# fp16 granule pipeline carried from the feed-forward part back to the mLSTM input block

## The chip, the cores and the metric

The kernel runs on one core of one Trainium2 chip. The metric is the device time of one execution in microseconds (us); lower is better. Times of the kernel before: 1895.95, 1896.54 and 1900.0 us, median 1896.54 us. The engines are named as in the profile: PE is TensorE (PEld its weight loads), DVE is VectorE, ACT is ScalarE, POOL is GpSimd, SP is SyncE, from whose queue most weights are fetched.

## The reference

One inference step of one decoder layer for 288 tokens (256 of a prompt, 8 samples of 4), in fp32. The mixer projects the normed input with one wide matrix `w_in` into three parallel branches (RG-LRU, gated linear attention, mLSTM) and into three merge gates, and adds the branches' outputs behind their gates. A squared-ReLU MLP follows.

```python
xn = rmsnorm(x, P['g_norm1']) * (1.0 + sc1) + sh1
proj = xn @ P['w_in']     # 2048 x 12312: lru_x, g_q, g_k, g_v, g_lr, g_gate, m_x, m_o, m_if, mg
y_lru, y_gla, y_ml = ...  # the three recurrences
gate = jax.nn.sigmoid(mg).reshape(B, T, 3, 2048)
merged = gate[:, :, 0] * (y_lru @ P['w_br_lru']) + gate[:, :, 1] * (y_gla @ P['w_br_gla']) \
       + gate[:, :, 2] * (y_ml @ P['w_br_ml'])
x = x + gt1 * (merged @ P['w_out'])
xn = rmsnorm(x, P['g_norm2']) * (1.0 + sc2) + sh2
x = x + gt2 * (jnp.square(jax.nn.relu(xn @ P['w_ff1'])) @ P['w_ff2'])
y = rmsnorm(x, g_final)
```

The shifts, scales and gates `sh1 ... gt2` are products of 9 conditioning rows with `w_ada` (2048 x 12288). The recurrences' new states are outputs too.

## The kernel before

**Layout.** Features lie on the 128 partitions, the 288 tokens along the free dimension. A weight matrix is read in granules: one fetch of 512 KB, a tile of 128 x 1,024, which holds eight 128x128 weight tiles. Every weight and every activation is split into a high and a low part, and each product takes three matmuls (high-high, high-low, low-high), so a granule is 24 matmuls of 128x288.

**Two ways to split.** Up to `wout` the function `stream` (L152 to L192) does it in fp32r: ACT copies the raw granule to `hi` (L160), DVE subtracts it to give `lo` (L162), PE multiplies at L169. It holds three raw, three high and three low tiles. The feed-forward part uses fp16 parts instead, which need a common power-of-two scale for each block of four granules. The class `Block` (L226 to L264) has the steps: `scan` squares a raw granule on ACT and adds it up (L236); `total` sums over the partitions with a ones product on PE into a PSUM bank of its own (L240); `scale` turns the sum into a power of two and its inverse with four small DVE operations (`power_of_two`, L195 to L202) and one that multiplies in the activations' factor (L245); `convert` makes the high part on ACT (L249) or on DVE (L251) and the low part on DVE (L252); `multiply` is L263. The factor is taken out again when the block's PSUM bank is evicted. The feed-forward loop scans ten granules ahead and converts three ahead; fetched granules lie in eleven places.

**Order.** The engines' instructions are put in order when the program is built, by priorities; `in_order` ties a granule step's instructions to the order in which they are written, `issue_after` ties one to another, and SP's queue follows the program. Work beside the streams (the recurrences as Python generators) advances by one piece after each granule (`run`, L272 to L283), and `finish` forces what is left of a piece of work.

**Stages**, with the start in the profiled execution: norm and the LRU, query, key and value blocks (0), the GLA output gate (218), merge 0 (272: four times a gate block and an output block, with LRU and then GLA beside it), the mLSTM input block (485), merge 1 (541, with mLSTM beside), the mLSTM output block (750), merge 2 (806), `wout` (982), feed-forward part (1088). Merge 1 and 2 multiply the gate by the branch's product and add (L1329, L1330); `wout` is evicted by `resid` (L1764 to L1769). At the start of the feed-forward part `second_norm` (L1815 to L1826) makes the 16 tiles of the normed input one by one; each serves the first block as soon as it is there.

**Conditional weights.** The products with `w_ada` are laid between the granules by a schedule written as a string (`every`). One half of each of the shift, scale and gate of the second norm is split into fp16 parts by `cond_parts` (L403 to L450; L411 and L417 on ACT, L419 on DVE, products at L433); the rest are fp32 products (L372).

Of the kernel before, what the change touches and what calls it, by code (L numbers as in the profile page):

```python
# [50 lines left out]
B_LRU, B_Q, B_GATE, B_MX, B_MO, B_MG = 0, 2, 6, 8, 10, 12  # L51
# [3 lines left out]
def trunk(ctx, tc, io):  # L55
# [22 lines left out]
    def slot(i, dt=F32):  # L78
        return big.tile([P, 8, N], dt, tag=f"s{i}", name=nm(f"s{i}"))
# [31 lines left out]
    junk = con[:, 0:512].bitcast(BF16)  # L111
# [40 lines left out]
    def stream(w, blk, act, kt, evac, g0=0, width=512, ahead=True, k0=0, kg=2, behind=None, banks=None):  # L152
# [3 lines left out]
        for g in range(k0 // kg, kt // kg):  # L156
# [28 lines left out]
            for m in range(nm_t):  # L185
# [3 lines left out]
                if g == kt // kg - 1:  # L189
                    with tc.high_priority():  # L190
                        evac(m, pss[m][:, :N])
            yield  # L192


    def power_of_two(p, n, of):  # L195

        q, t, u = (of[:, i:i + 1] for i in (4, 5, 6))
        V.tensor_reduce(out=q, in_=p[:, 0:n], axis=AX.X, op=ALU.add)
        V.tensor_scalar(q.bitcast(I32), q.bitcast(I32), 0x7F000000, 1, ALU.bitwise_and, ALU.logical_shift_right)
        V.tensor_scalar(u.bitcast(I32), q.bitcast(I32), -1, 204 << 23, ALU.mult, ALU.add)  # L200
        V.tensor_scalar(t.bitcast(I32), q.bitcast(I32), 50 << 23, None, ALU.add)
        return t, u  # L202

# [15 lines left out]
    taken = {"n": 0}  # L219

    def bank():

        taken["n"] += 1
        return longp() if taken["n"] % 5 == 0 else pm.tile([P, 512], F32, tag="mm", name=nm("mm"))

    class Block:  # L226

        def __init__(self, w, blk, g0, width, act, back, evac, by_act):
            self.w, self.blk, self.g0, self.act, self.back, self.evac, self.by_act = w, blk, g0, act, back, evac, by_act
            self.nm_t, self.kg = width // P, 1024 // width  # L230
            self.of, self.ps = None, None

        def scan(self, g, raw):
            if g == 0:
                self.of = sc([P, 8], "sums", 4)
            pace["hi"] = S.activation(junk, raw, AF.Square, accum_out=self.of[:, g:g + 1])  # L236

        def total(self):
            self.p = misc()
            T.matmul(self.p[:, 0:4], words(ones, 1, BF16), words(self.of[:, 0:4], 1, BF16), start=True, stop=True)  # L240

        def scale(self):
            t, self.u = power_of_two(self.p, 4, self.of)
            self.c = self.of[:, 7:8]
            V.tensor_tensor(out=self.c, in0=t, in1=self.back(), op=ALU.mult)  # L245

        def convert(self, g, raw, hi, lo):
            if g in self.by_act:
                pace["hi"] = S.activation(hi, raw, AF.Copy, scale=self.u)  # L249
# [3 lines left out]

        def multiply(self, g, hi, lo, ms, kks):
            if self.ps is None:
                self.ps = [bank() for _ in range(self.nm_t)]
# [1875 lines left out]
```

## Time and profile before

| | |
|---|---|
| median of the three runs | 1896.54 us |
| the profiled execution's own time | 1895.68 us |
| its span, first to last instruction | 1893.9 us |
| busy share of the span: PE, DVE, ACT, POOL | 98%, 67%, 59%, 12% |
| granted PE clock, mean | 0.995 |
| moved by DMA | 422.90 MB, 223 GB/s |

Busy time of PE is a union of overlapping instructions: matmuls are pipelined, so the length of one (286 to 301 ns in the groups) is not the time that it adds. The time between two starts is that, and the chain of waits shows it as a length and a count. "L169" is line 169 of the kernel. A row of a window has its start and end, its length, then each engine's busy time and its number of instructions, the granted clock, the DMA engines' busy share and GB/s. A row of waits has who waited for whom, the total, the number and the longest.

### The profile page before, as it was taken

The numbers are of one execution on the slowest core, as the hardware profiler recorded it, in microseconds if no ns is written. First come the engines' busy times: TensorE is split into PE (matmuls) and PEld (weight loads), VectorE is DVE, ScalarE is ACT, GpSimd is POOL, SyncE is SP. The second block draws the span as 40 slices with busy tenths as digits, with TensorE's granted clock in tenths as the row PEclk, the third lists the DMA queues.
The fourth block names the chain that finished last, engine by engine and source line by source line (L and its number), as shares of the span: only waits on it lengthen the run. The fifth ranks groups of instructions, "written<-read, shape, count | busy, mean of one in ns | idle before, by whom it ended". The sixth has DMA issues, their size and how long they took to land.

```text
span 1893.9 us, 38893 instructions
## 1 busy us (share of the span) xinstructions
PE 1847.8 (98%) x15874; PEld 1621.6 (86%) x15874; DVE 1268.2 (67%) x2239; ACT 1117.3 (59%) x1861; POOL 219.9 (12%) x302
## 2 busy tenths in 40 slices
PE   8999999999999999999999979999999999999997
PEld 7998889999999999999999947777777777777775
DVE  4767846645684557776558678776868676767676
ACT  5333374545454444566448568877777766666673
POOL 0001200000123010011101520000000000000091
PEclk9999999999999999999999999999999999999999
DMA  9998666547844358856787656565556555556541
GB/s 384 398 372 301 242 236 240 201 145 260 276 159 168 134 172 296 302 204 223 296 341 298 246 210 222 172 222 185 189 188 203 176 181 168 188 169 188 168 155 51
DMA packets 113442, 422.90 MB, mean 223 GB/s; under 512 B 11808, under 2 KB 12096, under 8 KB 110064
## 3 DMA queue, kind: packets, MB, share of 16 engines
q1 hardware_dynamic: 97040, 361.04, 54.9%
q0 software_dynamic: 11472, 42.79, 6.4%
q10 hardware_dynamic: 4752, 16.60, 2.2%
q8 instruction: 124, 2.03, 0.4%
q14 instruction: 54, 0.44, 0.1%
HBM read 403.56 MB, written 16.81 MB: 222 GB/s over the span
## 4 chain that ended last, share of the span: by engine, by line
PE 80%; DVE 9%; ACT 6%; issue 3%; DMA 1%; POOL 0%; SPq 0%; DVEq 0%; ACTq 0%; POOLq 0%
PE mm L169 39%; PE mm L263 24%; PE pi L263 6%; PE pa L372 3%; DVE pair L252 2%; ACT pair L249 2%; PE px L169 2%; DVE lo L162 1%; ACT con L236 1%; DMA raw<-win 1%; ACT hi L160 1%; PE pa L433 1%; DVE pair L251 0%; DVE s L800 0%; PE px L1649 0%
## 5 line engine op out<-in xcount | busy, mean ns | idle before, releaser
L263 PEld LDWEIGHTS <-pair 128*128 128x128 f16 x6144 | 596.6, 98 | 176.8 <-issue 11.9
L160 ACT ACTIVATE hi<-raw 128x1024 fp32r<-128x1024 f32 x272 | 286.9, 1057 | 407.4 <-PE mm L169 250.4
L162 DVE TENSOR_TENSOR lo<-raw,hi 128x1024 fp32r<-128x1024 f32 x272 | 334.9, 1233 | 248.0 <-ACT hi L160 227.9
L169 PE MATMUL mm<-xh,hi 128*128 128x288 f32 x1440 | 429.4, 301 | 4.0 <-ACT xh L718 1.7
L169 PE MATMUL mm<-xl,hi 128*128 128x288 f32 x1440 | 423.5, 297 | 0.0
L169 PE MATMUL mm<-xh,lo 128*128 128x288 f32 x1440 | 411.9, 296 | 2.0 <-DVE lo L162 1.9
L263 PE MATMUL mm<-x,pair 128*128 128x288 f16 x2448 | 316.1, 287 | 10.1 <-ACT x L1824 6.3
L263 PE MATMUL mm<-hx,pair 128*128 128x288 f16 x2472 | 321.8, 286 | 2.7 <-ACT s L1873 1.4
L169 PEld LDWEIGHTS mm<-xh,hi 128*128 128x128 f32 x1440 | 270.4, 188 | 15.8 <-issue 8.1
L169 PEld LDWEIGHTS mm<-xl,hi 128*128 128x128 f32 x1440 | 270.8, 188 | 1.4
L169 PEld LDWEIGHTS mm<-xh,lo 128*128 128x128 f32 x1440 | 266.0, 188 | 4.9 <-DVE lo L162 2.9
L169 PE MATMUL mm<-s,hi 128*128 128x288 f32 x1280 | 252.8, 297 | 1.1 <-DVE s L1769 0.7
L169 PEld LDWEIGHTS mm<-s,hi 128*128 128x128 f32 x1280 | 201.8, 188 | 5.1 <-issue 2.9
L169 PE MATMUL mm<-s,lo 128*128 128x288 f32 x640 | 179.2, 296 | 1.6 <-DVE lo L162 1.0
L252 DVE SCALAR_TENSOR_TENSOR pair<-xl,sums,pair 128x1024 f16<-128x1024 f32 x92 | 117.8, 1284 | 62.9 <-ACT pair L249 61.6
L252 DVE SCALAR_TENSOR_TENSOR pair<-s,sums,pair 128x1024 f16<-128x1024 f32 x92 | 118.1, 1284 | 52.7 <-ACT pair L249 51.4
L252 DVE SCALAR_TENSOR_TENSOR pair<-raw,sums,pair 128x1024 f16<-128x1024 f32 x72 | 93.2, 1295 | 41.6 <-ACT pair L249 40.6
L169 PEld LDWEIGHTS mm<-s,lo 128*128 128x128 f32 x640 | 116.9, 188 | 2.3 <-DVE lo L162 2.1
L1861 POOL TENSOR_SCALAR s<-s,mod 128x256 f32<-128x256 f32 x16 | 21.5, 1347 | 675.7 <-DVE s L1877 675.7
L236 ACT ACTIVATE con<-s 128x1024 bf16<-128x1024 f32 x92 | 96.3, 1046 | 1.3 <-DMA s<-wf 0.3
L236 ACT ACTIVATE con<-xl 128x1024 bf16<-128x1024 f32 x92 | 96.2, 1046 | 0.9
L263 PE MATMUL pi<-hx,pair 128*128 128x288 f16 x600 | 89.8, 286 | 3.1 <-DVE rs_t L1767 1.8
(526 smaller groups left out, 2275.7 us busy)
## 6 DMA issues: line engine op xcount, KB each, us to landing
raw<-win SPq DMA_DIRECT2D x192, 512.0 KB, 4.4
s<-wf SPq DMA_DIRECT2D x92, 512.0 KB, 3.9
xl<-wf SPq DMA_DIRECT2D x92, 512.0 KB, 4.1
raw<-wf SPq DMA_DIRECT2D x72, 512.0 KB, 3.9
s<-wq SPq DMA_DIRECT2D x20, 1024.0 KB, 8.7
raw<-wout SPq DMA_DIRECT2D x32, 512.0 KB, 5.9
s<-wada SPq DMA_DIRECT2D x13, 1024.0 KB, 7.3
ag<-wada POOLq DMA_DIRECT2D x12, 1024.0 KB, 7.8
```

The source lines that it names most:

```text
L160: pace["hi"] = S.activation(hi, raw, AF.Copy)
L162: pace["lo"] = V.tensor_tensor(out=lo, in0=raw, in1=hi.bitcast(F32), op=ALU.subtract)
L169: pace["last"] = T.matmul(ps, w[:, kk, ms], x, start=k == k0 and i == 0, stop=k == kt - 1 and i == 2)
L236: pace["hi"] = S.activation(junk, raw, AF.Square, accum_out=self.of[:, g:g + 1])
L249: pace["hi"] = S.activation(hi, raw, AF.Copy, scale=self.u)
L252: pace["lo"] = V.scalar_tensor_tensor(lo, raw, self.u, hi, ALU.mult, ALU.subtract)
L263: pace["last"] = T.matmul(self.ps[m][:, :N], a[:, kk, m * P:(m + 1) * P], x, start=k == 0 and i == 0, stop=k == 4 * self.kg - 1 and i == 2)
L372: pace["prod"] = T.matmul(ps[32 * j:32 * j + 32, h * w // 4:(h + 1) * w // 4], stat(k), v[:, j], start=k == 0 and h == 0, stop=k == kt - 1 ...
L433: pace["prod"] = T.matmul(ps[32 * j:32 * j + 32, a:a + 256], c, v[:, j], start=q == i == n == 0, stop=q == KT // each - 1 and n == 1, skip ...
L1861: G.tensor_scalar(a[:, 0:NP], a[:, 0:NP], mod[:, GT2, k, 0:1], None, ALU.mult)
```

## The change

The pipeline of `Block` now starts 40 blocks earlier. One list holds all blocks from the mLSTM input on: 4 of the mLSTM input, then merge 1 (two gate blocks of 256 columns and one output block of 512, four times), 4 of the mLSTM output gate, merge 2 like merge 1, 8 of `wout`, and the feed-forward blocks. `feed` runs through it: in each granule step it converts up to seven granules ahead and scans up to twelve (fourteen in the feed-forward part).

- The normed input `xn` is converted from its fp32r parts to fp16 parts in four groups (`halves16`: POOL adds the parts to one tile, ACT and DVE split it again), beside the first output blocks of merge 0. The buffers of the fp32r parts are cut up so that each can be given on.
- Merge 0 first does all four gate blocks, then all four output blocks. During these sixteen granules, still in fp32r, `ramp` fetches, scans and converts the first granules of the pipeline.
- The branch results and the merged sum are measured and split into fp16 parts (`measured`, `measured_sum`, `merged`) instead of fp32r parts.
- `total` writes into columns 288 and up of the first bank of the block that is being multiplied, between the products of its first and second output tile; in the feed-forward part it keeps a bank of its own.
- The first two feed-forward blocks are multiplied side by side, tile by tile (`by_k`).
- `cond_parts` is gone: all conditional weights are fp32 products. The GLA and the LRU recurrence are one generator, LRU no longer forced after the first gate block.

The core of the diff, shortened:

```diff
-    def stream(w, blk, act, kt, evac, ..., banks=None):
+    def stream(w, blk, act, kt, evac, ..., banks=None, then=None):
...
+            if then:
+                then(g, pss)
             yield
...
         def total(self):
-            self.p = misc()
-            T.matmul(self.p[:, 0:4], words(ones, 1, BF16), words(self.of[:, 0:4], 1, BF16), start=True, stop=True)
+            p = None
+            if pipe["now"]:
+                p = pipe["now"][0][:, N + 4 * pipe["col"]:N + 4 * pipe["col"] + 4]
+                pipe["col"] += 1
+            self.p = rows_total(self.of, 4, p)
...
+    def pipe_convert(to):
+        pipe_scale()
+        to = min(to, 4 * pipe["totals"] - 1, pipe["converted"] + 1)
+        while pipe["converted"] <= to:
+            i = pipe["converted"]
+            b, g = pipe["blocks"][i // 4], i % 4
+            tag = ("uh", "hi", "lo")[i % 3]
+            t = (wp if i % 3 else sp).tile([P, 2048], F16, tag=tag, name=nm("pair"), bufs=3)
...
+            b.convert(g, raw, *pipe["pairs"][i])
...
+            pipe_fetch()
...
+    def feed(count, act, evac, back, factor=1.0, pre=None, by_k=None, late=False):
+        if by_k:
+            two = pipe["blocks"][s // 4:s // 4 + 2]
+            for g in range(4):
...
+                        pipe_convert(s + (7, 9, 10, 11)[g])
+                        pipe_scan(s + 2 * g + pipe["scan"])
+                    for kk in range(two[0].kg):
+                        for i, b in enumerate(two):
+                            b.multiply(g, *pipe["pairs"][s + 4 * i + g], range(b.nm_t), (kk,))
...
+        for j in range(2 if by_k else 0, count):
+            for g in range(4):
...
+                        if g == 0:
+                            b.start(act, back() if callable(back) else back, factor)
+                            pipe.update(now=b.ps if pipe["total"] == 12 else None, col=0)
...
+                        if not last:
+                            pipe_convert(s + 7)
+                            pipe_scan(s + pipe["scan"])
+                    for m in ms:
+                        b.multiply(g, *pipe["pairs"][s], (m,), kks)
+                        if pipe["now"] and m == 0 and g < 3:
+                            pipe_total((s + pipe["total"]) // 4)
+                        if g == 3:
+                            with ahead():
+                                evac(j * b.nm_t + m, b.ps[m][:, :N], b.c)
...
+    def ramp(b):
+        def then(g, pss):
+            s = 4 * b + g
...
+                pipe_fetch()
+                if s > 5:
+                    pipe_scan(2 * s - 11)
+                if s > 8:
+                    pipe_convert(0)
+                if s > 7 and g == 0:
+                    pipe_total(1)
...
+    def merge_first():
+        for b in range(4):
...
+            run(stream(win, B_MG0 + b, act1, KT, lambda m, p: S.activation(gts[b][:, m, :], p, AF.Tanh, scale=0.5)))
...
+        while not ylru:
+            next(lru_)
+        beside(halves16())
+        for b in range(4):
...
+            run(stream(io["wbl"], b, lambda k: (ylru[0][:, k, :], ylru[1][:, k, :]), 8, ev, then=ramp(b)))
...
-    for b in range(2):
-        run(stream(win, B_MX + b, act1, KT, to_slot(mx, 4 * b)))
+    run(feed(4, act_x, lambda m, p, c: S.activation(mx[:, m, :], p, AF.Copy, scale=c), back1))
...
-            run(stream(w, b, lambda k: (y[0][:, k, :], y[1][:, k, :]), 8, ev))
+            run(feed(1, lambda k: (y[0][:, 0, k, :], y[0][:, 1, k, :]), ev, lambda: y[1],
+                     pre=lambda c: S.activation(gt, gt, AF.Identity, bias=c, scale=c)))
...
-        run(stream(io["wout"], b, act_m, KT, ev_o))
+    run(feed(6, act_m, ev_o, z[0][:, 5:6], 0.5))
...
+    run(feed(2, act_m, lambda m, p, c: ev_o(12 + m, p, c), z[0][:, 5:6], 0.5, late=True))
```

742 lines of the change are left out of this document (406 added, 336 removed).

## The prediction

> **What bounds the kernel now.** I read the page first, then the chain of waits by window, then busy time by stage, then PE's waits. The page says that TensorE (PE) is busy nearly all the time:
>
> ```profile
> span 1893.9 us, 38893 instructions
> PE 1847.8 (98%) x15874; PEld 1621.6 (86%) x15874; DVE 1268.2 (67%) x2239; ACT 1117.3 (59%) x1861; POOL 219.9 (12%) x302
> ```
>
> So time can only leave through fewer or faster matmuls, or through the few stretches in which PE stands. The chain shows how fast each kind of matmul runs when nothing holds it (start, length, engine, line, count):
>
> ```profile
> 1059.22 25.54 PE mm L169 x192
> ...
> 1556.51 10.29 PE mm L263 x84
> ```
>
> L169 is the fp32r product of `stream`, L263 the fp16 product of `Block.multiply`; both move 128x288. They take 25.54/192 = 133.0 ns and 10.29/84 = 122.5 ns apiece. The stretches, with the stages that the change touches: mLSTM input and the tail of GLA (485 to 580), merge 1 and the mLSTM output block (580 to 806), merge 2, `wout`, the start of the feed-forward part (1088 to 1125), and what follows:
>
> ```profile
> core 0: us, PE busy (x) PEld busy (x) DVE busy (x) ACT busy (x) POOL busy (x), PEclk, DMA share, GB/s
> 485.00:580.00 95.00, 94.36 (x761) 88.53 (x760) 70.66 (x115) 50.03 (x72) 27.27 (x42) 1.00 0.62 206
> 580.00:806.00 226.00, 226.00 (x1922) 214.14 (x1922) 136.67 (x269) 107.73 (x183) 20.48 (x39) 1.00 0.64 217
> 806.00:982.00 176.00, 175.09 (x1449) 169.12 (x1449) 107.46 (x153) 95.60 (x139) 22.59 (x16) 1.00 0.71 261
> 982.00:1088.00 106.00, 103.32 (x901) 99.05 (x900) 77.89 (x151) 77.93 (x122) 34.10 (x32) 1.00 0.75 282
> 1088.00:1125.00 37.00, 26.13 (x195) 15.31 (x188) 27.06 (x59) 20.39 (x51) 12.34 (x31) 0.91 0.51 192
> 1125.00:1330.00 205.00, 201.64 (x1693) 160.33 (x1692) 147.98 (x255) 166.59 (x309) 0.00 (x0) 1.00 0.61 204
> ```
>
> PE is full in all but the one from 1088 to 1125, where it has only 195 matmuls in 37 us. PE's waits agree:
>
> ```profile
> PE mm L263 <- ACT x L1824: 6.3, 8, 2.0
> PE mm L169 <- DVE lo L162: 2.9, 4, 1.0
> PE px L240 <- ACT con L236: 2.1, 3, 1.0
> PE mm L263 <- POOL x L1826: 1.6, 8, 0.3
> PE mm L263 <- ACT s L1873: 1.4, 2, 0.7
> PE pi L263 <- DVE s L1877: 1.4, 3, 1.0
> PE mm L169 <- DVE s L1769: 0.7, 1, 0.7
> PE mm L169 <- DVE ue L412: 0.6, 1, 0.6
> ```
>
> **1. Pace.** 160 granules of 24 matmuls go from fp32r to fp16 parts: 16 of the mLSTM input, 48 of each of the merges 1 and 2, 16 of the output block, 32 of `wout`. That is 3,840 matmuls, as many as before, each 10.5 ns shorter: **-40.3 us**. They stand on the path, PE being full there.
>
> **2. Start of the feed-forward part.** The first products wait for the normed tiles:
>
> ```profile
> L1825 DVE SCALAR_TENSOR_TENSOR x<-row,mod,x x16: 482/484/573, 1093.6 to 1119.4; 128x256 f16<-128x256 f32 x16
> ```
>
> 16 tiles come out in 26.3 us, 1.6 us each, while one block uses only 6 x 122.5 ns = 0.74 us of PE per tile. With `by_k` two blocks share each tile, 1.47 us. So 96 more matmuls lie under the norm: -11.8 us. The waits of L240 in this window go too, since sums are then ahead:
>
> ```profile
> PE px L240 <- ACT con L236: 1.7, 2, 1.0
> ```
>
> Against that, four granules are converted between the tiles where three were: one more conversion, +1.9 us (4., below) of VectorE (DVE), which makes the tiles. Together **-11.6 us**. The clock row, 0.91 here, says that gaps also cost clock; I count nothing for it.
>
> **3. Waits that go.** In `wout` (982 to 1088) the waits for L1769, L412 and this one, since evictions no longer meet the conditional weights' parts: 2.3 us.
>
> ```profile
> PE mm L169 <- DVE lo L162: 1.0, 1, 1.0
> ```
>
> Some of L1873 and L1877, for the same reason: 1.7 us of 2.8. **-4 us**.
>
> **4. What the granules cost beside PE.** The feed-forward stage already runs this way, so its rows price the new steps:
>
> ```profile
> L236 ACT ACTIVATE con<-s 128x1024 bf16<-128x1024 f32 x92 | 96.3, 1046 | 1.3 <-DMA s<-wf 0.3
> L236 ACT ACTIVATION_READ_ACCUMULATOR con<-s 128x1 f32 x92 | 17.2, 187 | 0.0
> L249 ACT ACTIVATE pair<-s,sums 128x1024 f16<-128x1024 f32 x46 | 52.4, 1138 | 37.4 <-DVE sums L201 31.0 <-DVE sums L200 4.1 <-DVE sums L245 2.1
> L251 DVE TENSOR_SCALAR pair<-s,sums 128x1024 f16<-128x1024 f32 x46 | 34.5, 750 | 0.0
> L252 DVE SCALAR_TENSOR_TENSOR pair<-s,sums,pair 128x1024 f16<-128x1024 f32 x92 | 118.1, 1284 | 52.7 <-ACT pair L249 51.4
> L198 DVE TENSOR_REDUCE sums<-px 128x1 f32<-128x4 f32 x64 | 10.0, 155 | 1.7 <-PE px L240 1.7
> L200 DVE TENSOR_SCALAR sums<-sums 128x1 int32<-128x1 int32 x64 | 9.8, 154 | 2.2
> ```
>
> ScalarE (ACT): 1.046 + 0.187 + half of 1.138 = 1.80 us a granule. DVE: 1.284 + half of 0.750 + a quarter of five small operations of about 0.155 = 1.85 us, where fp32r granules cost it 1.23. PE needs 24 x 122.5 ns = 2.94 us. Taking the old conversions out of the stages:
>
> ```profile
> 485.00:580.00 95.00, 33.49 (x27) 1.00 0.62 206
> 580.00:806.00 226.00, 63.98 (x54) 1.00 0.64 217
> ```
>
> (L162 on DVE.) From 485 to 580 other DVE work is 70.66 - 33.49 = 37.2 us; 27 new conversions make 50.0, and raising the lead from four ready pairs to eight 7.4 more: 94.6 us, against 95 - 27 x 0.252 = 88.2 us of PE. From 580 to 806: 72.7 + 54 x 1.85 = 172.6 against 212.4. So DVE is short only at the start, by 6 us, and what comes later has room; four pairs ahead are 11.8 us of cover, and the lead need not be built at once. I take +3 us, between 0 and 7.4; this takes in the ramp in merge 0, whose scans, sums and sixteen fp16 tiles of x lie under 16 fp32r granules. ACT has room everywhere.
>
> The 40 new sums on PE cost a weight load and a 4-column product each, nearly hidden:
>
> ```profile
> L240 PEld LDWEIGHTS <-ones x44: 97/98/98, 1339.0 to 1851.1; 128*128 128x128 bf16 x44
> ```
>
> At most 40 x 0.1 = 4 us, at least 0; **+1.5 us**. The conditional halves go back to fp32 products, at the same PE price:
>
> ```profile
> 1084.77 3.36 PE pa L372 x57
> ...
> 1539.19 0.99 PE pa L433 x32
> ```
>
> 8 x 59 = 0.47 us a unit against 16 x 31 = 0.50: nothing. That their scaling leaves ACT and DVE is the room used above.
>
> **5. The added wait.** The sum of a block is now written into a free column of the bank that PE is filling, right after the first output tile's products of a granule, and DVE reads it (L198) before PE may write that bank again. Before, each sum had a bank of its own, so no row shows such a wait. PE has the other tile's products in between, 12 x 122.5 ns = 1.47 us; the read needs 0.155 and whatever stands ahead of it on DVE. If that is one 1.284 or less, nothing is late. If a `hi`, a `lo` and an eviction stand there, 1 us is. What waits behind PE's matmul is every later matmul. Below zero it cannot go: no wait is taken away in exchange but the 2.1 us already counted. Ends: 0 and 40 x 1 = 40 us; I take 0.2 us a block, **+8 us**, nearer the low end because the sum's rows before show DVE reading 155 ns pieces with 1.7 us of idle ahead of 64 of them.
>
> The Trainium skill ("PSUM — Partial Sum Buffer", "Summary: rules for kernel authors") speaks against this edit: reading a bank while matmuls run, one should target another bank and guard by bank, not by address. By that rule every one of the 40 sums is a hand-over from PE to DVE and back; no run shown here has one.
>
> **6. Order and queues.** The four gate blocks of merge 0 now precede its outputs, so LRU need not be forced after the first; PE was full there, 0. Each SP fetch goes out as a conversion frees its place, two steps (5.9 us) ahead of its scan:
>
> ```profile
> raw<-win SPq DMA_DIRECT2D x192, 512.0 KB, 4.4
> raw<-wout SPq DMA_DIRECT2D x32, 512.0 KB, 5.9
> ```
>
> That covers the usual landing, barely in `wout`; a late one holds ACT's queue, evictions included, but seven converted granules stand between. 0.
>
> **Sum.** -40.3 - 11.6 - 4 + 3 + 1.5 + 8 = -43.4 us. The profiled execution took 1895.68 us (span 1893.9 and 1.8 around it): 1852.3; the median shown is 0.9 above it, so **1853 us**.
>
> **Rivals.**
> - *DVE sets the pace through the shared bank (chance 0.2).* The mLSTM and GLA steps put pieces ahead of the read, the lead of eight no longer helps since PE meets DVE once a block: 0.7 us in each of 40 blocks, 28 instead of 8, and the 6 us short at the start in full: 1876 us. For it: the 94.6 against 88.2 us. Against: from 580 on DVE has a fifth free.
> - *Nothing new waits (0.2).* Terms 4 and 5 near 0, and the clock of 1088 to 1125 comes back, 37 x 0.09 = 3.3 us: 1853 - 12.5 - 3.3 = 1837 us; and where fp32r runs as below, 22.57/168 = 134.3 ns, term 1 is 5 us more, and it ends near 1832.
>
> ```profile
> 905.03 22.57 PE mm L169 x168
> ```
>
> - *Slower (0.06).* The same hand-over, with the whole chain in series: PE waits for scan, read and scale of each block because ACT and DVE lag a step behind. The savings less terms 4 are 51 us, so the point is 51/40 = 1.3 us a block; a lag of one `scan` (1.23) plus a `lo` (1.28), less the 1.47 of cover, is 1.04, and with an eviction of a second more 2: 40 x 2 = 80, 1925 us. Against: DVE and ACT have 20% and more left in most stages.
> - *The pace does not change (0.04).* If 133.0 ns came from what runs beside, not from the kind of operand, term 1 is lost: 1893 us. Against: the 192 matmuls at 133.0 and the 84 at 122.5 are both unbroken. The Trainium skill ("TensorE: Matmul & The Clock Gate", "Wait — 56ns, not 53.3ns?") gives columns over 2.4 GHz plus 2.5 ns with no term for the operand, 122.5 ns for 288 by estimate; the fp16 row agrees, the fp32r row does not, and by it the sum would keep only terms 2 to 5.
>
> **How the numbers follow.** The forecast has 0.5. Its own range is 1845 to 1863 (term 5 from 0 to 18). 1828 to 1885 holds it with the free case and the shared-bank case (up to 0.9 us a block) and leaves out the two ends. 0.2%, 3.8 us, is what a measurement here can tell: faster 0.90, within it 0.04, slower 0.06.
>
> **What would show it.** Right: fp16 matmuls at 122.5 ns from the mLSTM input on; no PE gap at the norm over 1 us after the first tile; few waits of PE for the read of the sums. Wrong: PE waiting for `sums` or `pair` 40 times with half a microsecond or more, DVE above 95% in merge 1, or gaps before the first fp16 granule.

## The result, and the profile after

The changed kernel takes 1945.0 us (median of four runs, 1941.1 to 1948.8), the kernel before on the same chip 1896.7 (1896.0 to 1900.0): 1.0251 times as long, 95% interval 1.0225 to 1.0277. The forecast was 1853 us, its range 1828 to 1885: 43 us less were forecast, 48 us more came.

The page after, top lines. TensorE has lost busy time (1847.8 us before), but its share fell from 98% to 95%:

```profile
span 1947.0 us, 39207 instructions
PE 1841.9 (95%) x15919; PEld 1495.5 (77%) x15919; DVE 1283.5 (66%) x2382; ACT 1144.2 (59%) x1969; POOL 223.4 (11%) x315
```

The chain of waits after, two unbroken runs of granule matmuls (start, length, line, count), in merge 1 and in the feed-forward part. They take 4.43/36 = 123.1 and 11.78/96 = 122.7 ns a matmul, so the faster pace is there:

```profile
743.43 4.43 PE mm L290 x36
...
1711.17 11.78 PE mm L290 x96
```

Busy time by stage after. Stages are cut where TensorE starts their first granule: all that lies ahead of the mLSTM input block, that block, merge 1, mLSTM output block, merge 2, `wout`, the first two feed-forward blocks, the rest:

```profile
core 0: us, PE busy (x) PEld busy (x) DVE busy (x) ACT busy (x) POOL busy (x), PEclk, DMA share, GB/s
0.00:498.50 498.50, 468.80 (x4303) 434.70 (x4304) 304.73 (x544) 237.05 (x369) 63.74 (x91) 0.98 0.72 266
498.50:563.70 65.20, 62.87 (x556) 44.58 (x556) 51.37 (x111) 48.26 (x92) 5.12 (x12) 0.97 0.73 265
563.70:772.70 209.00, 199.17 (x1725) 154.28 (x1724) 144.87 (x304) 132.16 (x236) 44.59 (x67) 0.97 0.57 190
772.70:841.20 68.50, 63.48 (x568) 46.54 (x567) 50.69 (x121) 36.33 (x67) 4.16 (x7) 0.95 0.85 300
841.20:1009.60 168.40, 158.88 (x1391) 120.38 (x1390) 111.25 (x197) 106.43 (x170) 10.07 (x13) 0.98 0.68 237
1009.60:1132.80 123.20, 111.99 (x978) 82.94 (x977) 81.53 (x168) 62.64 (x107) 19.55 (x23) 0.97 0.71 258
1132.80:1172.50 39.70, 27.70 (x194) 20.00 (x194) 22.64 (x50) 20.23 (x48) 22.77 (x45) 0.87 0.31 113
1172.50:1947.00 774.50, 748.96 (x6216) 592.12 (x6214) 516.40 (x893) 501.10 (x884) 53.35 (x59) 0.99 0.53 176
```

The same cuts before (first and last lie at 0 to 484.1 and 1140.4 to 1893.9). Two things are to be seen. TensorE's clock, the third number from the right, was 0.99 or 1.00 in all stages but the last one shown, and now is 0.95 to 0.98 in the first six. And DVE is nowhere near full after:

```profile
484.10:546.80 62.70, 62.70 (x515) 57.69 (x514) 43.00 (x78) 32.34 (x49) 8.27 (x18) 1.00 0.68 230
546.80:748.40 201.60, 200.96 (x1661) 192.02 (x1660) 121.13 (x211) 96.84 (x158) 36.39 (x60) 1.00 0.55 183
748.40:811.90 63.50, 63.50 (x557) 58.97 (x556) 46.96 (x101) 31.12 (x50) 3.23 (x6) 1.00 0.89 303
811.90:978.90 167.00, 166.09 (x1385) 160.75 (x1385) 103.23 (x148) 93.70 (x137) 22.59 (x16) 1.00 0.69 257
978.90:1105.40 126.50, 119.28 (x1036) 109.47 (x1035) 91.19 (x184) 85.28 (x142) 40.09 (x46) 0.99 0.78 293
1105.40:1140.40 35.00, 27.69 (x196) 19.38 (x195) 25.25 (x43) 26.61 (x60) 6.35 (x17) 0.94 0.42 147
```

The next table splits each difference by TensorE's own record: a matmul's time is from its start to the start of the next. Where that is over 0.4 us, a matmul of a granule is counted at its normal length and the rest is a gap; of another matmul, what goes beyond 0.5 us is a gap. "Forecast" is terms 1 to 3 of the prediction; its terms 4 and 5 put 12.5 us on top.

| stage | before, us | after, us | forecast | came | granule matmuls | other matmuls | gaps |
|---|---|---|---|---|---|---|---|
| up to the mLSTM input | 484.1 | 498.5 | 0 | +14.4 | - | -2.6 | +17.0 |
| mLSTM input | 62.7 | 65.2 | -4.0 | +2.5 | -3.1 | +3.3 | +2.4 |
| merge 1 | 201.6 | 209.0 | -12.1 | +7.4 | -12.0 | +10.0 | +9.5 |
| mLSTM output | 63.5 | 68.5 | -4.0 | +5.0 | -2.4 | +2.6 | +4.9 |
| merge 2 | 167.0 | 168.4 | -12.1 | +1.4 | -11.3 | +3.2 | +9.3 |
| `wout` | 126.5 | 123.2 | -10.4 | -3.3 | -7.3 | +1.5 | +2.5 |
| first two feed-forward blocks | 35.0 | 39.7 | -11.6 | +4.7 | +1.4 | -0.5 | +3.8 |
| rest | 753.5 | 774.5 | -1.7 | +21.0 | +6.6 | +7.0 | +7.4 |

(In the last row 39 matmul records of before are missing, 4.8 us, which stand there as gaps of before.) Every stage missed. With these records put in their place, the columns add up to -32.9 us for the granules' matmuls, +24.5 for the others and +61.6 for gaps. TensorE's waits after (who for whom, total, times, longest) name the places:

```profile
PE mm L290 <- DVE sums L201: 19.0, 13, 4.7
PE mm L170 <- ACT hi L161: 14.5, 3, 10.2
PE mm L290 <- ACT y L2074: 14.3, 3, 8.3
PE px L2090 <- ACT hs L2086: 11.2, 8, 1.5
...
PE mm L290 <- ACT s L1069: 4.3, 1, 4.3
PE pi L1885 <- DMA st<-mC: 2.7, 1, 2.7
PE pi L1885 <- DMA s<-mC: 2.4, 1, 2.4
```

Line numbers from here on are the changed kernel's: L201 is the read of a block's sum, L161 `stream`'s `hi`, L249 a scan, L290 a granule's matmul, L2074 a tile of the second norm, L2086 the sum over the hidden rows' squares, L1069 a half of a branch's output, L1885 the mLSTM state product.

**The theory that was put to the test (A):** the pace is gained, and lost again at several separate places where a piece of work that TensorE needs stands behind other work in the queue of SyncE, ACT, DVE or POOL. **Rivals:** the shared bank of the sums is the cause (B), or DVE is late there whatever the bank (C).

### The profile page after: what moved, and what is told of

The parts are those of the page before. It is cut to its first block, busy times and chain, and to the rows that moved or that the text cites. A ratio compares the mean times of both kernels' runs of the same rounds, so it can differ in the third digit from the quotient of the medians.

```text
span 1947.0 us, 39207 instructions
## 1 busy us (share of the span) xinstructions
PE 1841.9 (95%) x15919; PEld 1495.5 (77%) x15919; DVE 1283.5 (66%) x2382; ACT 1144.2 (59%) x1969; POOL 223.4 (11%) x315
## 4 chain that ended last, share of the span: by engine, by line
PE 76%; DVE 9%; ACT 6%; DMA 4%; issue 3%; POOL 2%; ACTq 0%; DVEq 0%; POOLq 0%
PE mm L290 45%; PE mm L170 13%; PE pi L290 7%; PE pa L503 4%; DVE pair L273 2%; PE px L170 2%; ACT xw L249 1%; DMA raw<-win 1%; ACT pair L270 1%; DMA xw<-win 1%; DVE pair L272 1%; DVE lo L163 1%; POOL s L2028 1%; DMA s<-mC 1%; ACT s L1239 1%
## 5 line engine op out<-in xcount | busy, mean ns | idle before, releaser
L290 PEld LDWEIGHTS <-pair 128*128 128x128 f16 x9984 | 971.6, 99 | 315.5 <-issue 58.8
L290 PE MATMUL mm<-y,pair 128*128 128x288 f16 x2448 | 315.7, 289 | 14.9 <-ACT y L2074 14.3
L290 PE MATMUL mm<-hx,pair 128*128 128x288 f16 x2472 | 321.2, 286 | 0.2 <-DVE rs_t L2018 0.2
L290 PE MATMUL mm<-x,pair 128*128 128x288 f16 x2304 | 303.2, 290 | 11.1 <-DVE sums L201 8.7
L273 DVE SCALAR_TENSOR_TENSOR pair<-xw,sums,pair 128x1024 f16<-128x1024 f32 x184 | 238.2, 1300 | 70.9 <-ACT pair L270 68.2
L161 ACT ACTIVATE hi<-raw 128x1024 fp32r<-128x1024 f32 x112 | 118.1, 1057 | 198.1 <-PE mm L170 112.1
L249 ACT ACTIVATE xw<-xw 128x1024 bf16<-128x1024 f32 x184 | 192.8, 1048 | 57.5 <-DMA xw<-win 23.7
L290 PE MATMUL mm<-s,pair 128*128 128x288 f16 x1536 | 201.3, 292 | 16.4 <-DVE sums L201 10.3
L163 DVE TENSOR_TENSOR lo<-raw,hi 128x1024 fp32r<-128x1024 f32 x112 | 138.9, 1242 | 103.4 <-ACT hi L161 97.5
L170 PE MATMUL mm<-xh,hi 128*128 128x288 f32 x672 | 199.2, 302 | 5.0 <-DVE xl L770 1.7
L170 PE MATMUL mm<-xl,hi 128*128 128x288 f32 x672 | 196.4, 297 | 0.0
L170 PE MATMUL mm<-xh,lo 128*128 128x288 f32 x672 | 187.5, 297 | 0.6 <-DVE lo L163 0.5
L249 ACT ACTIVATE xw<-raw 128x1024 bf16<-128x1024 f32 x137 | 143.6, 1048 | 34.0 <-DMA raw<-win 11.9
L2109 POOL TENSOR_SCALAR s<-s,mod 128x256 f32<-128x256 f32 x16 | 23.2, 1453 | 681.2 <-DVE s L2122 681.2
L249 ACT ACTIVATE xw<-s 128x1024 bf16<-128x1024 f32 x88 | 92.1, 1046 | 14.1 <-DMA s<-wf 13.3
```

Source lines behind the costliest of these rows:

```text
L161: pace["hi"] = S.activation(hi, raw, AF.Copy)
L163: pace["lo"] = V.tensor_tensor(out=lo, in0=raw, in1=hi.bitcast(F32), op=ALU.subtract)
L170: pace["last"] = T.matmul(ps, w[:, kk, ms], x, start=k == k0 and i == 0, stop=k == kt - 1 and i == 2)
L249: pace["scan"] = S.activation(pipe["junk"], raw, AF.Square, accum_out=self.of[:, g:g + 1])
L273: pace["lo"] = V.scalar_tensor_tensor(lo, raw, self.u, hi, ALU.mult, ALU.subtract)
L290: pace["last"] = T.matmul(self.ps[m][:, :N], a[:, kk, m * P:(m + 1) * P], x, start=k == 0 and i == 0, stop=k == 4 * self.kg - 1 and i == 2)
```

## The experiments

The profile of one execution carries an uncertainty of its own: the mLSTM output block took 68.5 us after, and 62.7, 71.0 and 72.7 in the second, third and fourth run, which differ from the changed kernel elsewhere. So medians of four executions or more decide about the time, and stages about the mechanism.

**1. Sums in a bank of their own.**

```diff
-pipe.update(now=b.ps if pipe["total"] == 12 else None, col=0)
+pipe.update(now=None, col=0)
...
-            if g == 0:
-                pipe.update(now=pss, col=0)
```

> Every block's scan sum gets a PSUM bank of its own again, as it had before the change; all else stays as changed. Theory A (several pieces of work that TensorE needs stand behind other work in the queues, and the shared bank is one of four such places): the 19.0 us of waits for the reduction of the sums go, and with them the half-speed stretches of the clock right behind the longest of them (6.8 us near 595, 725 and 1019, 3.4 near 520, half of each lost: some 12 us); so 1945 - 31 = about 1914 us if none of it comes back elsewhere, 1930 if half does. Rival B (the shared bank is the cause of the loss): back to or below the 1897 us of before. Rival C (DVE is late whatever the bank; TensorE will wait for the conversions instead): 1940 to 1950 us, with waits for pair tiles of 15 us in place of those for sums.

1944.3 us, 1.0257 times before (1.0239 to 1.0274): nothing gained. In merge 1 (209.1 us, 209.0 after) TensorE's waits changed their names. The changed kernel there:

```profile
PE mm L290 <- DVE sums L201: 8.4, 3, 4.7
PE mm L213 <- ACT xw L249: 1.2, 1, 1.2
```

and with banks apart, where (in this run's own line numbers) L1558 is an eviction by DVE and L1543 one by ACT:

```profile
PE mm L290 <- DVE t L1558: 4.0, 1, 4.0
PE mm L290 <- ACT ag L1543: 2.4, 1, 2.4
PE px L1861 <- DVE s L1224: 1.7, 1, 1.7
```

B falls. C has the time right and the cause in part: TensorE waits all the same, but for evictions and not, as C said, for conversions. What stands ahead of the read is seen in the changed kernel's DVE timeline (start, length, line): 14 pieces of the mLSTM convolution (L919) in a row, six more, conversions between and behind them, and the read (L201) of a sum only at 597.4. Its product on TensorE had started at 590.5, and TensorE stands from 592.9 to 597.6:

```profile
586.30 5.59 DVE L919 SCALAR_TENSOR_TENSOR s<-s,par,s 128x255 f32<-128x255 f32 x14
...
593.88 2.44 DVE L919 SCALAR_TENSOR_TENSOR s<-s,par,s 128x255 f32<-128x255 f32 x6
...
597.44 0.14 DVE L201 TENSOR_REDUCE sums<-mm 128x1 f32<-128x4 f32 x1
```

**2. The parts of x given on later.** In the ramp, the two buffers of x's low parts were offered to the granule fetches at steps 5 and 6, before POOL had read them for the last time. SyncE's queue after:

```profile
441.28 0.81 SPq L301 DMA_DIRECT2D xw<-win  x2
442.19 0.37 SPq L160 DMA_DIRECT2D raw<-wbl  x1
453.21 0.81 SPq L301 DMA_DIRECT2D xw<-win  x2
454.11 15.38 SPq L160 DMA_DIRECT2D raw<-wbl  x7
```

Between 442.6 and 453.2 SyncE issues nothing: it waits for the second buffer, and merge 0's own weights (`wbl`) stand behind. Ahead of 441.3 it had stood for the first buffer, 27.5 us long. Both times POOL's reading of x's parts (L833) ends the wait:

```profile
SPq L301 <- POOL t L833: 38.1, 2, 27.5
```

TensorE pays 10.2 us for these weights:

```profile
451.08 2.29 PE L170 MATMUL mm<-s,hi 128*128 128x288 f32 x8 [10.18 <-ACT hi L161]
```

```diff
-                if s == 5: ... places += views(xlw[0])
-                if s == 6: ... places += views(xlw[1])
+                if s == 8: ... places += views(xlw[0])
+                if s == 9: ... places += views(xlw[1])
```

> The two tiles that held x's low parts are offered to the granule fetches three steps of the ramp later, so that their fetches stand behind three more fetches of the first merge's own weights on SP's queue. Theory A: the 10.2 us wait at 440 and the 1.0 and 3.4 us behind it (waits for a conversion whose raw tile was fetched late) go, and most of the 17 us at half speed behind them (8 us lost): 1945 - 20 = about 1925 us. Rival (the wait comes from the four scans, the sixteen halvings and the conversions that ACT has to do in these 20 us, whatever SP's order): 1942 to 1945 us, the same wait of ACT's conversion at 440 to 460.

1936.6 us (1.0211; 1.0189 to 1.0234): 8 us, not 20. The stage is 8.8 us shorter (489.7), the 10.2 us wait is gone, but one of 5.4 for a `hi` is left: SyncE still stood for the buffers until 442.7 and 454.2, 21.6 us in all in place of 38.1, and ACT has sixteen halvings and four scans in these 20 us.

**3. The hidden rows' sums in order.** ACT's timeline after: the sum (L2086) that TensorE waits for stands behind two conversions and a scan:

```profile
1249.14 1.13 ACT L270 ACTIVATE pair<-s,sums 128x1024 f16<-128x1024 f32 x1
1250.18 1.04 ACT L249 ACTIVATE xw<-raw 128x1024 bf16<-128x1024 f32 x1
...
1251.22 1.13 ACT L270 ACTIVATE pair<-raw,sums 128x1024 f16<-128x1024 f32 x1
1252.26 0.19 ACT L2086 ACTIVATE hs<-hs 128x8 f32<-128x8 f32 x1
```

```diff
-            hidden_rows(hb)
+            with in_order(), ahead():
+                hidden_rows(hb)
```

> The eight sums over the squares of the hidden rows are issued in the granules' order, ahead of the next granule's conversion and scan, instead of behind them. Theory A: the eight waits of TensorE of 1.69 us each go: 1945 - 13.5 = about 1931 us. Rival (the next conversion that this pushes back, or the sum's own chain, is waited for instead): 1943 to 1945 us with as many waits at the same places.

1935.4 us (1.0212; 1.0194 to 1.0230). All eight waits are gone, the rest of the feed-forward part fell from 774.5 to 759.2 us. Of these 15 us the median shows 10.

**4. Conditional weights out of slots 6 and 7.** POOL's scaling of x (L2028) for the second norm starts at 1125.8 us after, though its data are ready at 1105. It writes slots 6 and 7, which hold conditional weights (`s`) that PE multiplies (L503) only then. First PE's timeline, then POOL's, after:

```profile
1124.59 1.93 PE L503 MATMUL pa<-s,silc 128*32 128x256 f32 x32
```

```profile
1125.79 4.66 POOL L2028 TENSOR_SCALAR s<-s,mod 128x256 f32<-128x256 f32 x4 [12.34 <-DVE s L2020]
```

(The profile names DVE as releaser. That it was PE's reading of the slots is shown by the run below, where the slots are all that changes.)

```diff
-slots.update(ids=("xh", "xh", 8, 9, None, "st", 6, 7, ...
+slots.update(ids=("xh", "xh", 8, 9, None, "st", 2, 9, ...
```

> Two of the conditioning-weight tiles of the output projection's stage lie in slots 2 and 9 instead of 6 and 7, so that GpSimd's scaling of x for the second norm, which writes slots 6 and 7, need not wait until those weights are multiplied at 1126 us. Theory A: GpSimd starts scaling near 1105 instead of 1126 us, the waits of 8.3 and 3.2 us at the start of the feed-forward part go with some 5 us of half-speed clock: 1945 - 14 = about 1931 us. Rival (the second norm's own chain over ACT and DVE sets the start; or the scaling then takes GpSimd from the sums of squares): 1940 to 1945 us, TensorE still waiting for y tiles for 8 us or more in all.

POOL now starts at 1110.0 us, and the first two feed-forward blocks take 30.7 us in place of 39.7, below the 35.0 of before. But `wout` gets 3.5 us longer (TensorE waits 1.5 us for the sum of squares, L667, and 3.31 for the first tile in place of 2.95), and the median is 1941.9 us (1.0249; 1.0223 to 1.0274): not told apart from the changed kernel. The two stages together take 157.4 us in place of 162.9; in the six later runs with this edit they take 153.0 to 160.0, in the other versions 157.3 (banks apart) to 163.7. So the mechanism is shown, and 5.5 us in these stages; in the median of this run alone no gain shows.

**5. The four together.** 

> The four edits together: sums in a bank of their own, the two tiles of x's low parts offered three steps later, the hidden rows' sums in the granules' order, conditioning weights out of slots 6 and 7. If the four places are independent, the stages that each edit shortened add up: ahead of the mLSTM block 499 to 490 us, output projection 123 to 117, first two feed-forward blocks 40 to 31, the rest 774 to 759, so 1945 - 9 - 6 - 9 - 15 = about 1906 us. If each freed wait only lets TensorE run into the next late piece (as the second edit's median did, 8 us for 14 us of waits): about 1920 us or more. Under neither theory does it reach the 1853 us of the forecast: the 27 us that the other matmuls took longer (conditioning products foremost) and the mLSTM side work's waits stay.

1918.6 us (1.0115; 1.0100 to 1.0130). 26 us are back, less than the stages of the single runs add up to (39): `wout` takes 122.3 us here against 117.2 in the first run, merge 2 172.3 against 168.4.

**6. The kernel before with all conditional weights in fp32**, one part of the change alone. (The second part of the edit empties the step of the schedule that made the halves.)

```diff
-        if parts:
+        if False:
             return cond_parts(name, load, 2, ...)
...
-                with tc.issue_after(pace["hi"].ins), tc.issue_after(pace["lo"].ins):
-                    next(...)
+                pass
```

> The kernel before with one part of the change alone: all the conditioning weights are multiplied as fp32, none in two fp16 halves, so that ScalarE's and VectorE's work on the halves goes and the 384 fp16 products (11.7 us of TensorE in the profile of before) become 384 fp32 ones at the pace of the others (97.2 us for 2,000: 18.7 us with some of the waits in them; 73.3 for 1,616 in before: 17.4 us). Theory D (these products are on TensorE's path at full length; the forecast's 'conditional halves: 0' was wrong): 1896.5 + 6 to 12, so 1902 to 1909 us. The forecast's theory (paid back by what ScalarE and VectorE no longer do): 1893 to 1898 us.

1900.8 us (1.0026; 1.0015 to 1.0037): 4 us slower. TensorE spends 95.4 us on these products in place of 85.0, of which 6 don't show in the time; that the ease on ACT and DVE gives them back is likely, not shown. Both theories were half right.

**7. The mLSTM convolution, one tile in two granule steps.**

```diff
             conv_tile(x, y, w, b, m)
             yield
+            if x is not lx:
+                yield
```

> The changed kernel with the mLSTM convolution's eight tiles issued one in two granule steps instead of one in each, so that fewer of its VectorE pieces stand in a row ahead of the granules' reduction, conversion and eviction. Theory A' (it is these side pieces on VectorE, not the bank, that hold TensorE at 589 to 597 us: 1.3 and 4.9 us of waits with 3.4 us of clock behind them): these waits go, the first merge's stage falls from 209 to about 202 us: 1945 - 7 = 1938 us. Rival (VectorE is short over the whole stage, and the pieces are waited for wherever they stand): 1943 to 1947 us, waits of as much in all, a few us later.

1940.8 us (1.0236; 1.0206 to 1.0266), not told apart from the changed kernel. Merge 1 falls from 209.0 to 193.4 us, close to the 189.5 of the forecast, and its clock is back at 1.00. But merge 2 grows from 168.4 to 176.1, since the mLSTM chain now ends eight granules later. A part of both is work that only moved: merge 1 has 1639 matmuls in place of 1725, which are 6.8 us less beside the granules, and merge 2 has 1453 in place of 1391, 6.7 us more. By stage (merge 1, output block, merge 2):

```profile
564.50:757.90 193.40, 187.42 (x1639) 148.14 (x1637) 133.40 (x266) 125.97 (x220) 40.21 (x62) 1.00 0.56 182
757.90:829.40 71.50, 65.47 (x594) 47.43 (x592) 55.10 (x127) 40.51 (x77) 5.29 (x10) 0.95 0.88 300
829.40:1005.50 176.10, 165.14 (x1453) 124.47 (x1450) 119.52 (x228) 107.97 (x175) 11.16 (x15) 0.96 0.72 249
```

**8. The end of the mLSTM branch issued before merge 2's first gate block.** `finish(ml_)` moved ahead of the two gate blocks. 

> The changed kernel with the end of the mLSTM branch (its last scalings, its measuring and its halves) issued before the last merge's first gate block instead of behind it. Theory A: the waits of 4.5 and 2.1 us for yml at 868 to 875 us go, and some 2 us of clock: 1945 - 8 = 1937 us. Rival (the branch's end is a chain of its own that is late, and now stands ahead of the granules' conversions, so that TensorE waits for these instead): 1943 to 1955 us, with waits for pair tiles near 840 to 850 us.

1947.1 us (1.0274; 1.0254 to 1.0295): no gain. The two waits for the branch's halves (4.3 and 1.8 us) are replaced by one for a scan that now stands behind that work, close to the rival's case:

```profile
PE mm L213 <- ACT xw L249: 7.7, 1, 7.7
```

**9, 11, 12. Edits 2, 3, 4 and 7 together; then with the extra step for every second tile only; then the ninth with x's low parts offered at steps 10 and 12.** The twelfth has one more edit: from step 8 on, the ramp may make a block's sum in every step, and not only in every fourth.

> Edits of the second, third, fourth and seventh runs together (x's low parts later, hidden sums in order, conditioning weights out of slots 6 and 7, the mLSTM convolution one tile in two steps), the sums staying in the blocks' banks. Theory A (each place costs what its stage showed): the stages ahead of the mLSTM block -9, first merge -15, first two feed-forward blocks -9, the rest -15, less the 8 us that the seventh run's later mLSTM chain cost in the last merge: 1945 - 40 = about 1905 us, and with the sums in the shared banks not slower than the fifth run (1919). Rival (the shared bank costs again what its own bank cost elsewhere; freed places collide): 1915 to 1920 us.

> As the ninth run, but only every second tile of the convolution gets the extra step, so that the mLSTM chain is pushed back by four granules in place of eight. If the chain's lateness at the last merge (waits of 5.0, 2.2 and 1.7 us near 860 us in the seventh run) is what eats the first merge's gain, some 4 us faster than the ninth run; if VectorE's pieces in a row still decide, slower by as much, with the wait for sums near 590 us back.

> As the ninth run, but the two tiles of x's low parts are offered at steps 10 and 12 of the ramp in place of 8 and 9. In the second run SyncE still stood at 442.7 and 454.2 us for them, and TensorE waited 1.6, 1.7 and 5.5 us for the first merge's own weights. If SyncE's order is all of it, these go and the stage ahead of the mLSTM block comes down to 484 us, as before the change: 5 us faster than the ninth run. If ScalarE's added halvings and scans are the rest, or the later fetches make the first granules late: no faster, with a wait for pair tiles near 490 us.

1913.4 (1.0088; 1.0061 to 1.0116), 1911.0 (1.0078; 1.0054 to 1.0101) and 1911.9 us (1.0074; 1.0050 to 1.0098); the three can't be told apart. The ninth lies between its two theories (1905, and 1915 to 1920). In the twelfth run SyncE stands only 5.3 us for the buffers, the stage up to the mLSTM input takes 477.4 us, 21 less than after and 12 less than in the ninth run, and from 430 us to its end TensorE waits once (1.4 us). But the mLSTM input, 65 to 66 us else, takes 73.6, with 5.1 us of waits for sums of the granules that came late: most of what the twelfth gains over the ninth in one place, it loses in the next.

**10. The changed kernel without 14 of the 16 stores of the mLSTM state.** 

> The changed kernel without 14 of the 16 stores of the updated mLSTM state (that output is not written; 7.2 MB less to move). Theory E (the mLSTM output block cannot gain from faster matmuls because its transfers bind: DMA busy 0.85 to 0.89 of the stage and 300 GB/s in both kernels, weights and state loads standing behind the stores): the two waits for mC loads (2.7 and 2.4 us) go, the stage falls from 68 to about 60 us, near its 60 us of matmuls; 1945 - 8 = 1937 us. Rival (GpSimd issues the loads too late, because their tiles come free only after the updates; the stores don't matter): the waits stay, 1943 to 1947 us.

1937.8 us (1.0215; 1.0198 to 1.0231), 7 us less, as theory E had it. The output block takes 59.6 us and TensorE is busy in all of it, at a clock of 1.00 and with 242 GB/s in place of 300:

```profile
773.20:832.80 59.60, 59.60 (x569) 44.97 (x568) 51.57 (x123) 35.59 (x66) 3.18 (x6) 1.00 0.69 242
```

So the stores hold this block back once its matmuls are faster: by their bytes, or by their landing, which the next load into the same tile waits for. The run doesn't separate the two, and how much they cost varies: with all stores the other versions take 61.8 to 72.7 us here.

**13, 14, 15. What is left in the merges.** The thirteenth is the eleventh with merge 2's conditional weights fetched two steps earlier (`" . L L L . . V"` for `" . . . L L L V"`); the fourteenth is the changed kernel without the convolution's DVE pieces; the fifteenth the thirteenth with x's low parts offered at steps 9 and 10.

> The eleventh run with the last merge's conditioning weights fetched two granule steps earlier in each round of seven, so that they have landed when TensorE comes to multiply them. Theory A (another placement that the faster granules outran): the waits of 1.2 and 0.8 us for these weights near 992 to 996 us go, and the 4.0 us wait for the sums right behind them with its half-speed stretch: 1911 - 6 = 1905 us. Rival (SyncE now waits longer for their tiles and holds the granules' own fetches): 1909 to 1920 us, TensorE waiting for scans whose raw tiles are late.

> The changed kernel without the 24 VectorE pieces of the mLSTM convolution (that convolution is left with its first tap, so the mLSTM outputs are other numbers; 10 us of VectorE's work are gone, no matmul). Theory A' (these pieces, in the queue ahead of reduction, conversion and eviction, make the first merge's loss): the waits at 589 to 610 us go, first merge 209 to 200 us or less, as in the runs that spread them out (194, 200), but with nothing pushed into the last merge: 1945 - 10 = 1935 us. Rival (the mLSTM chain is a chain of its own with the same end, and TensorE waits for it at the last merge): first merge shorter, last merge longer by as much, 1943 us or more.

> The thirteenth run with x's low parts offered at steps 9 and 10 of the ramp (between the eleventh run's 8 and 9 and the twelfth's 10 and 12, which took 12 us from the stage ahead of the mLSTM block and gave 8 back behind it). If the ramp's loss is only a matter of place there is a better one: 3 to 5 us less than the thirteenth run, about 1901 us. If what SyncE's order frees is always waited for in the granules' first conversions: the same as the thirteenth run, within 3 us. In neither case is the kernel before (1896) beaten for certain.

The thirteenth: 1911.7 us (1.0077; 1.0060 to 1.0094), no gain. The waits for these weights near 995 us shrank from 1.7 to 0.5 us, and the wait for the sums behind them grew from 3.8 to 5.5. The fourteenth: 1938.7 us (1.0222; 1.0198 to 1.0246), not clearly apart from the changed kernel, whose four executions it overlaps. Merge 1 takes 202.4 us, where all versions that leave the convolution alone take 208.5 to 209.1: 6 us less. That is not as much as spreading the pieces out gave (seventh run), which also moved other work. So the pieces on DVE do cost there. But merge 1, output block and merge 2 together still take 433.7 us, 30 above the 403.9 of the forecast, with 10 us of DVE work less. The fifteenth: 1912.1 us (1.0074; 1.0059 to 1.0089), as the thirteenth; its stage up to the mLSTM input takes 485.5 us, 4 less than the thirteenth's, and merge 2 takes 8 more. No version made here beats the kernel before.

## Why the prediction was wrong

The step that failed is the overlap. The prediction took the faster matmuls off the time in full, and gave all that they would newly wait for +11 us (terms 4 and 5, without the sums' own 1.5) and term 6 nothing. The granules' matmuls did get faster by 41.0 us. But TensorE's gaps grew by 61.6 us, its other matmuls by 24.5, and 8 us came back in single granule matmuls that took longer. Term by term:

- **1, pace: right.** -40.3 us were forecast; over the five stages the granule matmuls came from 510.4 to 469.4 us, -41.0, when single ones that took 0.2 to 0.4 us are counted at their normal length (the table counts them as they ran). The rival "the pace does not change" is out. The premise beside it failed: "they stand on the path, PE being full there". PE was full because it was the slowest; made 8% faster, it waited for ACT, DVE and the transfers, and through ACT for SyncE, at the places of the list of waits above.
- **2, start of the feed-forward part: wrong by 16 us** (-11.6 forecast, +4.7 came). The step priced DVE's tiles and left out POOL: the scaling that makes the tiles' input waited for conditional weights in its slots until 1126 us. Without that wait (fourth run) these blocks took 30.7 us, -4.3: two blocks to a tile do help, less than forecast, as TensorE still waits 2.3 us for a later tile. The gain did not show in that run's median. The clock that gaps cost, for which the term counted nothing, was 0.87 in this stage after.
- **3, waits that go:** the waits of `wout` named there are gone, but six for sums (5.5 us) and three others came, and `wout` gave 3.3 us in place of 10.4.
- **4, cost beside PE.** The sum over the stage ("94.6 against 88.2", "from 580 on DVE has a fifth free") was the wrong measure: DVE is busy 145 of 209 us in merge 1 and 51 of 65 in the mLSTM input, so it had room on the average, and was late all the same, because the order in its queue put side pieces and conversions, 20 of the convolution's alone near 590 us, ahead of one small read. And "8 x 59 = 0.47 us a unit": in the trace each fp32 product is two records of 59 ns, so a unit of 8 products is 16 records, 0.94 us. 24 units cost TensorE 12 us (85.0 to 97.2), half of what its other matmuls took longer, and not nothing; alone on the kernel before, 4 us of time. The new sums on PE were priced rightly: +1.5 us forecast, 1.3 came (2.3 to 3.6).
- **5, added wait: the size, not the cause.** 40 blocks at 0.2 us were forecast; 13 waits of 19.0 us in all came, the longest 4.7. But with the banks apart the time is the same, so the bank only lent its name to DVE's and ACT's lateness. To target another bank, as the Trainium skill's rule has it ("PSUM — Partial Sum Buffer", "Summary: rules for kernel authors"), changed nothing in the time here: 1944.3 against 1945.0 us.
- **6, order and queues: wrong, 0 forecast.** "Each SP fetch goes out as a conversion frees its place" left out the ramp, where places are buffers that POOL still reads. SyncE stood 38.1 us for two of them, and 14.4 us of the loss are ahead of the mLSTM input. The later the buffers are offered, the less SyncE stands and the shorter this stage: 38.1, 21.6, 18.2 and 5.3 us in the changed kernel and in the second, fifteenth and twelfth runs, with a stage of 498.5, 489.7, 485.5 and 477.4. (The last two have other edits as well, which act later, and the twelfth the one on the ramp's sums.) One of the prediction's own signs of being wrong came true here: gaps before the first fp16 granule. Nor was the order of `hidden_rows` looked at, issued outside `in_order`: eight waits, 11.2 us.
- **What no step looked at.** The mLSTM chain keeps its own length: it advances by one piece a granule, waits for its state loads in an output block that its stores hold back (tenth run), and its halves are due at merge 2. What merge 1 gains, merge 2 pays in part (seventh run); and with the branch's end moved ahead, a scan is late in its place (eighth).
- **Rivals.** "DVE sets the pace through the shared bank" was right in DVE's pieces ahead of the read, wrong in the bank and by 69 us. "Slower" had the right sign, not its mechanism: no scan, read and scale in series at each of 40 blocks, but a handful of long waits at places that differ.

**What is shown and what is not.** Shown in the median by taking them away: the order in the ramp (8 us), the hidden sums (10), the stores (7), the conditional products (4 on the kernel before); the first two with the fourth edit and a part of the seventh together 34. Shown in their stages alone: the slots (5.5 us) and the convolution's pieces (6 in merge 1). Not shown: what makes the last 14 us against the kernel before, in the eleventh run; that cause stays open. By stage this run is 5.2 us longer than the kernel before up to the mLSTM input, 2.9 in that block, 5.7 in merge 2 and 8.0 in the rest of the feed-forward part, and elsewhere as long or shorter. In that rest, where the granules were fp16 before as well, the conditional products took 3.9 us in fp16 before and take 10.1 in fp32. Each edit that removed some brought others. No run put a late read or eviction itself ahead of the side pieces in DVE's queue.

## What to carry to other kernels

Before counting a faster inner loop as gained, list for each stage what arrives just in time at the old pace: side chains that advance with the loop, fetches that wait for a buffer, small reads in queues behind long side work, transfers near the stage's rate. A busy share of 70% on a helper engine says nothing about one small operation that TensorE needs soon; look at the order in its queue. And take the count of a program's operation from the same record as its price: a price of one record times the number of instructions is wrong where one instruction makes two.

## What the runs showed of the hardware that was not expected

Behind a long wait TensorE runs slower for some microseconds. Windows of the changed kernel: before the 4.7 us wait at 592.9, in it, the 6.8 us behind it, and after these (the clock is the third number from the right):

```profile
585.00:592.60 7.60, 6.42 (x54) 5.00 (x52) 7.60 (x17) 6.22 (x12) 0.00 (x0) 1.00 0.45 140
592.60:597.60 5.00, 0.29 (x3) 0.10 (x1) 5.00 (x14) 2.39 (x3) 0.00 (x0) 0.80 0.31 105
597.60:604.40 6.80, 6.76 (x37) 4.58 (x37) 6.29 (x14) 5.35 (x8) 5.93 (x9) 0.64 0.28 85
604.40:611.00 6.60, 6.37 (x55) 5.24 (x52) 5.91 (x9) 2.85 (x5) 5.89 (x9) 1.00 0.63 213
```

37 matmuls where the next window of about that length has 55. A wait of 1.53 us (hidden rows, 1251 us) left the clock at 1.00, one of 2.16 us at 518 us was followed by a window at 0.51:

```profile
520.50:524.00 3.50, 3.45 (x15) 2.20 (x15) 2.77 (x9) 0.76 (x1) 0.50 (x3) 0.51 1.02 401
1252.50:1258.00 5.50, 5.40 (x45) 4.37 (x46) 4.37 (x8) 4.92 (x9) 0.00 (x0) 1.00 0.58 191
```

Over the sixteen profiles taken after the prediction, from 440 us to 20 us ahead of the end, the record of the granted clock shows how often. Counted are gaps between the starts of two matmuls that began at full clock. The clock was 0.5 within 2 us of the gap's end for all 53 gaps of 3.5 to 6 us, for 29 of 32 between 3 and 3.5 us, 33 of 83 between 2 and 3 us, and 9 of 104 between 1.5 and 2 us. The Trainium skill ("TensorE: Matmul & The Clock Gate", "Why this matters for your kernels") advises against idle gaps of more than about 3 us; the runs agree, and show that a shorter one isn't safe. The mean clock fell from 0.995 to 0.980. From the mLSTM input on, 144 of the granules' matmuls ran at half clock and took 0.2 to 0.4 us after, 16.9 us beyond their normal length in all; before, 21 did, 2.6 us. So half the clock cost some 14 us more on these matmuls, and the prediction counted nothing for it. (The 8 us of the section above are net: before, more of them took longer singly at full clock.)
